# Where two pieces of work stand at the entry of a halved FFN: values of two covered tiles, and ScalarE's copy of a bank

## The chip, the cores and the metric

The kernel runs on one core of one Trainium2 chip. The metric is the time of one execution on the device in microseconds (us), as the median of several executions; lower is better. Engines are called TensorE (PE in the profile: matmuls, PEld its weight loads), VectorE (DVE), ScalarE (ACT), GpSimd (POOL) and SyncE (SP, which issues most DMAs).

## The reference, cut to what matters

The reference is a two-layer decoder trunk on one sequence of 512 tokens with 1024 features, in float32. Each layer has two SwiGLU FFNs, one on each side of a block of three token mixers, so an execution runs four FFNs.

```python
D_MODEL = 1024
SEQ = 512
DEPTH = 2
D_FF = 2816

def rms_norm(x, gain):
    xf = x.astype(jnp.float32)
    inv = lax.rsqrt(jnp.mean(xf * xf, axis=-1, keepdims=True) + EPS)
    return (xf * inv).astype(x.dtype) * gain

def swiglu(h, w_in, w_out):
    gate, up = jnp.split(h @ w_in, 2, axis=-1)
    return (jax.nn.silu(gate) * up) @ w_out

    for l in range(DEPTH):
        x = x + 0.5 * swiglu(rms_norm(x, ffn1_norm[l]), ffn1_w_in[l], ffn1_w_out[l])
        ...
        x = x + y @ w_mix_out[l]
        x = x + 0.5 * swiglu(rms_norm(x, ffn2_norm[l]), ffn2_w_in[l], ffn2_w_out[l])
```

## The kernel before, in words

Every float32 product is made of three matmuls on rounded operands: an operand is split into a high part (rounded by ScalarE) and a low part, the remainder (a subtraction by VectorE), and `mm3` (L304) issues high times high, high times low of the moving side, low of the weights times high (L308, L314, L315).

An FFN has 22 tiles of 128 hidden features, taken in pairs, in three chunks of 8, 8 and 6 tiles (`CHUNKS`). The first `covered` tiles (6 in the first FFN, 4 in the others) are computed plainly, on x times the gain, while the norm is still being computed: `enter` (L541) does it for the last three FFNs, `cover` (L474) for the first. Their banks are taken out by `clear` (gate and up times the norm's factor `inv` on VectorE, then Silu on ScalarE) and `values` (two VectorE instructions per tile, L669 and L666, that multiply gate and up into the hidden tile `hq`).

All other tiles are computed by `halved` (L722) in a scheme with seven products, named P1 to P7, in place of eight (Strassen and Winograd's). A unit is one pair of tiles (kind "I", the input projection) or one half of the output projection of one of the first two chunks (kind "O"; the last chunk is projected plainly); there are 35 units of kind I in an execution. A product is 24 matmuls into one of three banks of its unit. In a unit of kind I the order is P1, P2, P6, P5, P7, P3, P4: P1, P6, P7 and P4 accumulate one after the other in bank a, P2 fills bank c, P5 and P3 accumulate in bank b. Between two products of a bank it has to be read:

- P1: ScalarE copies bank a, negated, to g1 (L865); P2: VectorE subtracts bank c from g1 (L868), ScalarE takes Silu;
- P6: ScalarE copies bank a, negated, to g2 (L872); P5: ScalarE copies bank b, negated, to u2 (L875);
- P7: VectorE adds bank a to u2 (L878); P3: VectorE adds bank b to g2 (L881), ScalarE takes Silu;
- P4: VectorE multiplies up the two hidden tiles out of g2, u2 and g1, bank a (L669, L666; L895, L896 in the last chunk).

So P6's copy must end before P7 can start, with P5 between; P5's copy before P3, with P7 between; and L878 before P4, with P3 between.

`plan` (L60) writes down one sequence of products per FFN: the first units of kind I alone, then I mixed with O. `LEAD` is 3: when product n has been issued, `prepare` rounds the weights (one granule of 128 x 1024, tile `hl`, three buffers) for product n+3 on ScalarE (L766), and hands back a function, `rest`, that has VectorE form the remainder (L768). This rounding writes the buffer that product n has just read. The body of the loop (L839 to L910) issues for each n: the product, the rounding of n+3, the reading of n's bank, `rest`, the list of sums and loads that the plan puts at n (`run(n)`; sums on VectorE L754, L780), and, in the first products of an FFN, one entry of `self.entry`, with which `enter` spreads its remaining work.

The order on each engine is the order in which these lines are issued: `follow` (L268) ties each of these instructions to the one before it on the same engine (`A` for ScalarE, `V` for VectorE). What `enter` does before the first halved product ends with the sum of the inputs of P7 (`add((0, 1), (1, 1))`), and `next(then)`, which lets `halved` go to its first products. The inputs of the products are formed by `high` (ScalarE, L589) and `low` (VectorE, L592 or L594) of tiles `xn`, into `xc`.

Of the kernel before, what the change touches and what calls it, by code (L numbers as in the profile page):

```python
# [13 lines left out]
AF = mybir.ActivationFunctionType  # L14
# [142 lines left out]
class Trunk:  # L157
# [377 lines left out]
    def values(self, fp, f, i, gi, ui, keep):  # L535
        V = (lambda i: self.follow("v", i)) if keep else (lambda i: i)
        a, k = divmod(f + i, 4)
        for b in range(2):
            V(self.hidden(self.quarter(fp, 0, a, b)[:, k, :], *(t[:, 256 * b : 256 * b + 256] for t in (gi, ui)), a != b))

    def enter(self, fp, w_in, then):  # L541
        nc = self.nc
        H = T // 2
        A, V = (lambda i, e=e: self.follow(e, i) for e in "av")

        def stream(f, banks, given):
            def parts(k, kk):
                r = slice(k * P, (k + kk) * P)
                return [w_in[r, f * P : (f + 2) * P], w_in[r, FF + f * P : FF + (f + 2) * P]]

            return self.stream_steps(
                [(bk, slice(c, c + P), None) for bk, c in zip(banks, (0, 256, 128, 384))],
                parts, self.xact, KD, given=given,
            )

        ba = self.next4()
        first = stream(0, ba, lambda k: k == KD - 2)
        for _ in range(4):
            next(first)
        nb = self.bank("pt" if self.ntog % 2 == 0 else "po")  # L560
        bb = self.next4()
        second = stream(2, bb, lambda k: True)
        self.ngain = self.const.tile([P, KD], F32, tag="ngain", name=self.n("ngain"))
        A(nc.scalar.activation(self.ngain, self.gain, AF.Copy, scale=-1.0))
        next(second)
        self.end_norm(nb, fp, True)
        self.table(SILU)
        next(first, None)
        next(then)
        X, self.xc, lows = {}, {}, {}  # L570

        def quarter(a, b):
            X[a, b] = t = fp.tile([P, 4, H], F32, tag=f"r{2 + 2 * a + b}", name=self.n("xn"))
            for k in range(4):
                i = 4 * a + k
                V(nc.vector.scalar_tensor_tensor(
                    out=t[:, k, :], in0=self.xT[:, i, b * H : (b + 1) * H],
                    scalar=(self.gain if a == b else self.ngain)[:, i : i + 1],
                    in1=self.inv[:, b * H : (b + 1) * H], op0=ALU.mult, op1=ALU.mult,
                ))  # L580

        def high(name):
            c = ORDER_IN.index(name)
            src, other = X[SUM[name]], name in NEGATIVE
            hi, lo = (
                fp.tile([P, 4, H], F32R, tag=f"x{w}{c}", name=self.n("xc")) for w in "hl"
            )
            self.xc[name] = hi, lo
            A(nc.scalar.activation(hi, src, AF.Copy, scale=-1.0) if other else nc.scalar.copy(hi, src))  # L589

            def low():
                V(nc.vector.scalar_tensor_tensor(  # L592
                    out=lo, in0=src, scalar=-1.0, in1=hi, op0=ALU.mult, op1=ALU.subtract
                ) if other else nc.vector.tensor_sub(lo, src, hi))  # L594

            lows[name] = low

        def add(x, y):
            V(nc.vector.tensor_add(X[x], X[x], X[y]))

        def both(name):
            high(name)
            lows[name]()

        def row():
            next(second)
            next(second, None)

        cleared = {}

        def clear(f, i):
            banks = bb if f else ba
            cleared[f, i] = self.clear(fp, banks[2 * i], banks[2 * i + 1], True)

        def values(f, i):
            self.values(fp, f, i, *cleared.pop((f, i)), True)

        quarter(0, 0)
        high("P1")
        quarter(1, 0)  # L620
        lows["P1"]()
        next(second)
        next(second)
        high("P2")
        quarter(0, 1)
        lows["P2"]()
        quarter(1, 1)
        next(second)
        next(second)
        add((0, 0), (0, 1))  # L630
        high("P5")
        clear(0, 0)
        lows["P5"]()
        next(second)
        next(second)
        next(second, None)
        add((0, 0), (1, 1))
        high("P6")
        self.given["total"]()
        lows["P6"]()  # L640
        self.given["prepare"](0)
        self.given["prepare"](1)
        clear(0, 1)
        add((0, 1), (1, 1))
        next(then)
        self.entry = {
            0: lambda: (high("P7"), values(0, 0), lows["P7"]()),
            1: lambda: (values(0, 1), high("P3")),
            2: lambda: (lows["P3"](), add((0, 0), (1, 0))),
            3: lambda: both("P4"),  # L650
            9: lambda: clear(2, 0),
            10: lambda: values(2, 0),
            12: lambda: clear(2, 1),
            13: lambda: values(2, 1),
        }
# [66 lines left out]
    def halved(self, fp, w_in, w_out, covered):  # L722
        nc = self.nc
# [3 lines left out]
        A, V, G, S = (lambda i, e=e: self.follow(e, i) for e in "avgs")  # L727
# [13 lines left out]
        def add(u, q, q2):  # L741
            G(nc.gpsimd.dma_start(raw[u, q], src(u, q2), accum_op=ALU.add))
# [70 lines left out]
        u = seq[0][:2]  # L813
# [25 lines left out]
        for n, (kind, w, p) in enumerate(seq):  # L839
# [3 lines left out]
            if p in new:  # L843
# [3 lines left out]
                u, p, acc, p in new, p in ("P2", "P3", "P4"),  # L847
                kind == "I" and p == "P1" and w in (covered, *(f0 for f0, _ in CHUNKS)),
            )
            rest = prepare(*seq[n + LEAD]) if n + LEAD < len(seq) else None  # L850
            if kind == "O":
                c, g = w

                for r, b, f in {
                    "P2": ((0, 0, -0.5),), "P1": ((0, 0, -0.5),), "P5": ((1, 1, -0.5),),
                    "P6": ((0, 1, -0.5),), "P7": ((1, 1, 0.5),), "P3": ((0, 1, 0.5),),
                    "P4": ((1, 0, 0.5),),
                }[p]:
                    xs = self.xT[:, 4 * r + 2 * g : 4 * r + 2 * g + 2, b * H : (b + 1) * H]
                    V(nc.vector.scalar_tensor_tensor(  # L860
                        out=xs, in0=pair(acc), scalar=f, in1=xs, op0=ALU.mult, op1=ALU.add
                    ))
            elif p == "P1":
                work[u, "g1"] = g1 = tmp("g1")
                A(nc.scalar.activation(g1, acc, AF.Copy, scale=-1.0))  # L865
            elif p == "P2":
                g1 = work[u, "g1"]
                V(nc.vector.tensor_sub(g1, g1, acc))  # L868
                A(self.act(g1, g1, AF.Silu))
            elif p == "P6":  # L870
                work[u, "g2"] = g2 = tmp("g2")
                A(nc.scalar.activation(g2, acc, AF.Copy, scale=-1.0))  # L872
            elif p == "P5":
                work[u, "u2"] = u2 = tmp("u2")
                A(nc.scalar.activation(u2, acc, AF.Copy, scale=-1.0))  # L875
            elif p == "P7":
                u2 = work[u, "u2"]
                V(nc.vector.tensor_add(u2, u2, acc))  # L878
            elif p == "P3":
                g2 = work[u, "g2"]  # L880
                V(nc.vector.tensor_add(g2, g2, acc))  # L881
                A(self.act(g2, g2, AF.Silu))
            else:
                g1, g2, u2 = (work[u, x] for x in ("g1", "g2", "u2"))
                c = next(i for i, (f0, nf) in enumerate(CHUNKS) if f0 <= w < f0 + nf)
                if c < 2:
                    a, k = divmod(w - CHUNKS[c][0], 4)
                    for b, g, v in ((1, g2, u2), (0, g1, acc)):
                        V(self.hidden(
                            self.quarter(fp, c, a, b)[:, k : k + 2, :], pair(g), pair(v), a != b  # L890
                        ))
                else:
                    q = (w - CHUNKS[c][0]) // 2
                    y = fp.tile([P, 2, T], F32, tag="S", name=self.n("y"), bufs=2)
                    V(nc.vector.tensor_mul(y[:, :, H:], pair(g2), pair(u2)))  # L895
                    V(nc.vector.tensor_mul(y[:, :, :H], pair(g1), pair(acc)))  # L896
                    hh, hl = (
                        fp.tile([P, 2, T], F32R, tag=f"r{t}", name=self.n("hh")) for t in tags[q]
                    )
                    self.hh.append(hh)  # L900
                    self.hl.append(hl)
# [718 lines left out]
```

## Time and profile before

| | |
|---|---|
| median of 3 runs | 1860.53 us (1856.95 to 1863.77) |
| profiled execution, its own time | 1854.12 us |
| its span, first to last instruction | 1852.3 us |
| TensorE clock granted | 1.00 |
| instructions | 33371 |

How to read the rows that follow. A row of the timeline has the start in us from the span's beginning, the duration, engine, line of the kernel, operation, output and input tiles (buffer numbers left out), shape, count, and in brackets how long the engine was idle before and what ended it. A row of the waits has who waited, for whom, us in total, how many times, and the longest. Rows of one engine overlap a little: an instruction starts before the last one has drained.

### The profile page before, as it was taken

To read this page: it belongs to the slowest core of one execution; us is meant where nothing else is said; L and a number is where in the kernel's file an instruction comes from. 1 tells how busy PE (TensorE), PEld (TensorE's weight loads), DVE (VectorE), ACT (ScalarE), POOL (GpSimd) and SP (SyncE) were. 2 spreads that over 40 slices of the span, in tenths; PEclk is the share of its full clock that TensorE was granted. 3 is DMA by queue.
4 is the path that set the end of the run, shared out by engine and by line. 5 is a ranking of instruction groups with operands and counts; after the bars stand their busy time and mean duration, and the time that the engine had idled before them with its cause. 6 is when DMAs were issued, how large, how long until landed. Compare 5 with 4: busy or idle time off the path is not lost.

```text
span 1852.3 us, 33371 instructions
## 1 busy us (share of the span) xinstructions
PE 1829.1 (99%) x13536; PEld 1700.0 (92%) x13536; DVE 1480.2 (80%) x2101; ACT 1007.3 (54%) x1467; POOL 177.3 (10%) x182
## 2 busy tenths in 40 slices
PE   8999999999999999999999999999999999999999
PEld 6899999899877899999889999998998788999997
DVE  7889787678787888878678887966868878888883
ACT  5455555564665555555445555545546664555552
POOL 0011120100000001112001111201000000020210
PEclk9999999999999999999999999999999999999999
DMA  7658783232223767868265787813323228577762
GB/s 205 171 121 190 182 176 96 69 95 73 75 75 97 209 131 170 186 170 171 81 200 127 163 192 185 171 59 90 81 64 87 80 91 228 148 160 194 150 136 91
DMA packets 245417, 251.90 MB, mean 136 GB/s; under 512 B 19568, under 2 KB 230000, under 8 KB 245264
## 3 DMA queue, kind: packets, MB, share of 16 engines
q1 hardware_dynamic: 191664, 183.69, 32.5%
q0 software_dynamic: 53600, 66.09, 22.3%
q8 instruction: 106, 1.74, 0.4%
q14 instruction: 47, 0.39, 0.1%
HBM read 223.98 MB, written 2.10 MB: 122 GB/s over the span
## 4 chain that ended last, share of the span: by engine, by line
PE 88%; DVE 6%; ACT 3%; issue 2%; DMA 1%; SPq 0%; ACTq 0%; DVEq 0%
PE mm L308 13%; PE mm L315 13%; PE mm L314 13%; PE sc L308 6%; PE sc L315 6%; PE sc L314 6%; PE pt L308 6%; PE pt L314 6%; PE pt L315 6%; PE po L308 3%; PE po L314 3%; PE po L315 3%; PE po L1472 1%; DVE hl L298 1%; PE pt L1513 1%
## 5 line engine op out<-in xcount | busy, mean ns | idle before, releaser
L766 ACT CAST hl<-w 128x1024 fp32r<-128x1024 f32 x322 | 337.2, 1049 | 317.2 <-PE mm L315 76.5
L768 DVE TENSOR_TENSOR hl<-w,hl 128x1024 fp32r<-128x1024 f32 x322 | 392.8, 1222 | 90.8 <-ACT hl L766 90.7
L298 DVE TENSOR_TENSOR hl<-st,hl 128x512 fp32r<-128x512 f32 (+2 forms) x196 | 166.5, 852 | 114.7 <-ACT hl L297 113.6
L297 ACT CAST hl<-st 128x512 fp32r<-128x512 f32 (+2 forms) x196 | 146.6, 750 | 184.8 <-PE mm L315 66.7
L308 PE MATMUL mm<-xc,hl 128*128 128x256 f32 (+1 forms) x732 | 201.7, 276 | 1.7 <-ACT g L872 1.4
L315 PE MATMUL mm<-xc,hl 128*128 128x256 f32 x728 | 201.4, 277 | 0.0
L314 PE MATMUL mm<-xc,hl 128*128 128x256 f32 x728 | 201.4, 277 | 0.0
L308 PE MATMUL sc<-xc,hl 128*128 128x256 f32 (+1 forms) x530 | 146.6, 277 | 2.4 <-ACT g L872 1.7
L315 PE MATMUL sc<-xc,hl 128*128 128x256 f32 x528 | 146.3, 277 | 0.0
L314 PE MATMUL sc<-xc,hl 128*128 128x256 f32 x528 | 146.2, 277 | 0.0
L308 PEld LDWEIGHTS mm<-xc,hl 128*128 128x128 f32 x732 | 137.4, 188 | 2.5 <-ACT g L872 1.8
L315 PEld LDWEIGHTS mm<-xc,hl 128*128 128x128 f32 x728 | 136.7, 188 | 0.1
L314 PEld LDWEIGHTS mm<-xc,hl 128*128 128x128 f32 x728 | 136.7, 188 | 0.0
L308 PE MATMUL pt<-xc,hl 128*128 128x256 f32 (+1 forms) x484 | 133.0, 276 | 0.0
L314 PE MATMUL pt<-xc,hl 128*128 128x256 f32 x480 | 133.0, 277 | 0.0
L315 PE MATMUL pt<-xc,hl 128*128 128x256 f32 x480 | 132.8, 277 | 0.0
L308 PE MATMUL mm<-hl,x 128*128 128x256 f32 (+1 forms) x384 | 112.3, 292 | 0.7 <-DVE qk L1403 0.3
L308 PE MATMUL mm<-x,hl 128*128 128x512 f32 x272 | 109.7, 403 | 0.0
L315 PE MATMUL mm<-hl,x 128*128 128x256 f32 (+1 forms) x384 | 107.4, 280 | 0.0
L314 PE MATMUL mm<-hl,x 128*128 128x256 f32 (+1 forms) x384 | 107.1, 279 | 0.0
L315 PE MATMUL mm<-x,hl 128*128 128x512 f32 x272 | 106.5, 392 | 0.0
L314 PE MATMUL mm<-x,hl 128*128 128x512 f32 x272 | 106.0, 390 | 0.0
(478 smaller groups left out, 5678.2 us busy)
## 6 DMA issues: line engine op xcount, KB each, us to landing
w<-in_ffn_w_in_dram SPq DMA_DIRECT2D x140, 512.0 KB, 5.5
w<-in_ffn_w_out_dram SPq DMA_DIRECT2D x64, 512.0 KB, 4.2
w<-in_ffn_w_out_dram POOLq DMA_DIRECT2D x56, 512.0 KB, 8.6
st<-in_w_mix_in_dram SPq DMA_DIRECT2D x88, 256.0 KB, 2.7
st<-in_ffn_w_in_dram SPq DMA_DIRECT2D x72, 256.0 KB, 3.1
w<-in_ffn_w_in_dram POOLq DMA_DIRECT2D x35, 512.0 KB, 8.5
w<-S POOLq DMA_DIRECT2D x35, 512.0 KB, 4.7
st<-in_ffn_w_out_dram SPq DMA_DIRECT2D x24, 512.0 KB, 3.6
```

The lines of the kernel that those rows point to most:

```text
L297: a = nc.scalar.copy(hi, src[:, c : c + w])
L298: b = nc.vector.tensor_sub(lo, src[:, c : c + w], hi)
L308: i = nc.tensor.matmul(acc[:, c], ah, bh[:, c], start=first and c.start == 0, stop=False, skip_group_check=True,)
L314: nc.tensor.matmul(acc, ah, bl, start=False, stop=False, skip_group_check=True)
L315: i = nc.tensor.matmul(acc, al, bh, start=False, stop=last, skip_group_check=True)
L766: A(nc.scalar.copy(hi, src))
L768: return lambda: V(nc.vector.tensor_sub(lo, src, hi))
L1472: nc.tensor.matmul(self.ob[:, t0 + u * P : t0 + 2 * P], V[:, j, h % 4].rearrange("p a d -> p (a d)"), part[:, j, u:, :].rearrange("p i t - ...
L1513: nc.tensor.transpose(tb[:, j * P : (j + 1) * P], p[:, j * P : (j + 1) * P], self.ident)
```

## The change

In `enter`, `values` of the second pair of covered tiles' first two tiles, (0, 0) and (0, 1), is issued before `next(then)`; before, it was part of the entries of products 0 and 1. With that, the input of P7 is formed in one piece after product 0, and the input of P3 in one piece after product 2, where its high part was issued after product 1.

In `halved`, the three copies of a bank by ScalarE (P1 to g1, P6 to g2, P5 to u2) are issued before `prepare` of product n+3, where they stood behind it. This holds for every unit of kind I, in all four FFNs.

```diff
@@ enter
         clear(0, 1)
         add((0, 1), (1, 1))
+        values(0, 0)
+        values(0, 1)
         next(then)
         self.entry = {
-            0: lambda: (high("P7"), values(0, 0), lows["P7"]()),
-            1: lambda: (values(0, 1), high("P3")),
-            2: lambda: (lows["P3"](), add((0, 0), (1, 0))),
+            0: lambda: both("P7"),
+            2: lambda: (both("P3"), add((0, 0), (1, 0))),
             3: lambda: both("P4"),
             9: lambda: clear(2, 0),
             10: lambda: values(2, 0),
@@ halved
+            out = {"P1": "g1", "P6": "g2", "P5": "u2"}.get(p) if kind == "I" else None
+            if out is not None:
+                work[u, out] = t = tmp(out)
+                A(nc.scalar.activation(t, acc, AF.Copy, scale=-1.0))
             rest = prepare(*seq[n + LEAD]) if n + LEAD < len(seq) else None
             if kind == "O":
                 c, g = w
@@
-            elif p == "P1":
-                work[u, "g1"] = g1 = tmp("g1")
-                A(nc.scalar.activation(g1, acc, AF.Copy, scale=-1.0))
+            elif out is not None:
+                pass
             elif p == "P2":
                 g1 = work[u, "g1"]
                 V(nc.vector.tensor_sub(g1, g1, acc))
                 A(self.act(g1, g1, AF.Silu))
-            elif p == "P6":
-                work[u, "g2"] = g2 = tmp("g2")
-                A(nc.scalar.activation(g2, acc, AF.Copy, scale=-1.0))
-            elif p == "P5":
-                work[u, "u2"] = u2 = tmp("u2")
-                A(nc.scalar.activation(u2, acc, AF.Copy, scale=-1.0))
             elif p == "P7":
                 u2 = work[u, "u2"]
                 V(nc.vector.tensor_add(u2, u2, acc))
```

## The prediction

> **What bounds the kernel now.** First the busy times of the page, then the list of what TensorE waited for.
>
> ```profile
> PE 1829.1 (99%) x13536; PEld 1700.0 (92%) x13536; DVE 1480.2 (80%) x2101; ACT 1007.3 (54%) x1467; POOL 177.3 (10%) x182
> ...
> PE sc L308 <- ACT g L872: 1.7, 2, 0.9
> PE mm L308 <- ACT g L872: 1.4, 2, 0.9
> PE sc L308 <- DVE u L878: 0.7, 2, 0.4
> PE mm L308 <- DVE u L878: 0.3, 1, 0.3
> ```
>
> TensorE is busy 99% of 1852.3 us; a change that removes no matmul can only close its gaps. The last four rows are all the waits that the halved products have for ScalarE's bank copies (L872, four times) and for VectorE's evacuation L878 (three times): once per FFN at its entry, for L878 in the last three FFNs only. They add up to 4.1 us of idle time, 0.2% of the span. So the upside is small from the start, and the question is what the new order makes late elsewhere.
>
> Second, the timeline of one entry (second FFN; the third and fourth repeat it), ScalarE, VectorE and TensorE in order of time.
>
> ```profile
> 650.70 0.59 ACT L865 ACTIVATE g<-sc 128x512 f32<-128x512 f32 x1
> 650.83 1.23 DVE L768 TENSOR_TENSOR hl<-w,hl 128x1024 fp32r<-128x1024 f32 x1 [1.62 <-ACT hl L766]
> 653.11 0.42 DVE L669 TENSOR_TENSOR hq<-gi,ui 128x256 f32<-128x256 f32 x1
> 653.78 1.22 DVE L592 SCALAR_TENSOR_TENSOR xc<-xn,xc 128x1024 fp32r<-128x1024 f32 x1
> 654.91 0.68 DVE L868 TENSOR_TENSOR g<-g,sc 128x512 f32<-128x512 f32 x1
> 655.63 0.64 ACT L262 ACTIVATE g<-g 128x512 f32<-128x512 f32 x1 [1.27 <-DVE g L868]
> 656.17 1.04 ACT L589 CAST xc<-xn 128x1024 fp32r<-128x1024 f32 x1
> 657.11 1.04 ACT L766 CAST hl<-w 128x1024 fp32r<-128x1024 f32 x1
> 657.55 0.28 PE L315 MATMUL pt<-xc,hl 128*128 128x256 f32 x1
> 658.05 0.59 ACT L872 ACTIVATE g<-sc 128x512 f32<-128x512 f32 x1
> 658.18 1.23 DVE L768 TENSOR_TENSOR hl<-w,hl 128x1024 fp32r<-128x1024 f32 x1 [0.78 <-ACT hl L766]
> 658.69 0.39 PE L308 MATMUL sc<-xc,hl 128*128 128x256 f32 x1 [0.87 <-ACT g L872]
> 663.95 0.68 DVE L878 TENSOR_TENSOR u<-u,sc 128x512 f32<-128x512 f32 x1
> 664.78 0.36 PE L308 MATMUL sc<-xc,hl 128*128 128x256 f32 x1 [0.35 <-DVE u L878]
> ```
>
> Starts give the steps, since an engine's rows overlap by some 0.1: 0.54 us for the Silu (655.63 to 656.17, its row is 0.64 long), 0.94 for a rounding (656.17 to 657.11), so 0.49 for a bank copy (0.59 less 0.10), and 0.67 for one call of values, two instructions (653.11 to 653.78). P7 accumulates into the bank that P6's copy reads. The last matmul before it starts at 657.55 and the rows around it are 0.11 apart, so P7 was wanted at 657.66 and came at 658.69: 1.03 lost, because the copy stood behind two roundings. P4 then waits for L878, which ends at 664.63; it starts 0.15 later.
>
> **The change, part by part.** No instruction is added or removed; TensorE, GpSimd and SyncE keep their order, and no DMA is moved. Two things move: in 35 units the three copies (P1, P6, P5) each go past one rounding on ScalarE, so a copy comes up to 0.94 sooner and that rounding up to 0.49 later; and in three entries 4 VectorE instructions of values (1.34 us) go ahead of the remainder of P6's granule, and the rounding of P3's input (656.17) goes behind two more ScalarE instructions. A copy put in front adds no wait on ScalarE: it waits for the end of its product, and the rounding behind it fills the buffer which that same product read. What stands behind the rounding is VectorE's remainder of it, and behind that the rest of VectorE's list; that is where the 0.49 can hurt. P3's input, 1.3 us later, is covered: its remainder came after VectorE's row of 658.18 in any case, and P3 follows P7 by a product.
>
> Entry of FFNs 2 to 4, the 1.03 at P7. VectorE idled 1.62 before its row at 650.83, waiting for the rounding that P1's copy now precedes: +0.49. One call of values no longer stands in front of L868: -0.67. L868 starts at 654.73, the Silu at 655.45, P6's copy right behind it at 655.99, done by 656.58, before 657.66. The wait is gone. The 1.34 us of values in front of P6's remainder fit into the 1.62 of idle time; without that they would cost P6 directly.
>
> The same entry, P4. P3's weights are now rounded at 656.48 instead of 657.11, so VectorE's row of 658.18 (it idled 0.78 there) moves to 657.55. From there to L878 VectorE runs without a pause, so L878 also moves by 0.63 and P4 starts at 664.15 instead of 664.78. Of the 1.03 only 0.63 are left; P4 waits 0.5 longer than it did.
>
> The next unit and a half. Here these rows decide.
>
> ```profile
> 679.34 0.63 ACT L262 ACTIVATE gi<-gi 128x512 f32<-128x512 f32 x1 [1.40 <-DVE gi L530]
> 679.88 1.03 ACT L766 CAST hl<-w 128x1024 fp32r<-128x1024 f32 x1
> 680.94 1.22 DVE L768 TENSOR_TENSOR hl<-w,hl 128x1024 fp32r<-128x1024 f32 x1 [1.04 <-ACT hl L766]
> 689.16 0.68 DVE L666 SCALAR_TENSOR_TENSOR hq<-g,pt 128x512 f32<-128x512 f32 x1
> 690.30 0.28 PE L308 MATMUL pt<-xc,hl 128*128 128x256 f32 x1
> ```
>
> The Silu at 679.34 hangs on VectorE, which by then runs only about 0.16 earlier (each copy-first slot eats 0.49 of the 0.63). Behind it P5's copy now comes before the rounding: 679.88 - 0.16 + 0.49 = 680.21. VectorE, idle there for 1.04, starts its row at 681.27 instead of 680.94 and runs without a pause to L666, which ends at 690.17 instead of 689.84. L666 empties the bank that P2 of the third unit takes. That P2 stood at 690.30, would be wanted at 689.67, and gets its bank at 690.17 + 0.15 = 690.32. The remaining gain is used up: +0.02 per entry, together **+0.1**. Bounds: if the 0.33 doesn't appear, -0.63 each; if the copies of that unit add a whole 0.49, +0.2.
>
> Entry of the first FFN, where values doesn't move.
>
> ```profile
> 86.13 1.23 DVE L768 TENSOR_TENSOR hl<-w,hl 128x1024 fp32r<-128x1024 f32 x1 [1.62 <-ACT hl L766]
> 91.55 0.63 ACT L262 ACTIVATE gi<-gi 128x512 f32<-128x512 f32 x1 [1.36 <-DVE gi L530]
> 92.08 1.03 ACT L766 CAST hl<-w 128x1024 fp32r<-128x1024 f32 x1
> 93.02 0.58 ACT L872 ACTIVATE g<-mm 128x512 f32<-128x512 f32 x1
> 93.66 0.39 PE L308 MATMUL mm<-xc,hl 128*128 128x256 f32 x1 [0.53 <-ACT g L872]
> 94.58 1.23 DVE L768 TENSOR_TENSOR hl<-w,hl 128x1024 fp32r<-128x1024 f32 x1 [0.20 <-ACT hl L766]
> 98.16 0.68 DVE L878 TENSOR_TENSOR u<-u,mm 128x512 f32<-128x512 f32 x1
> 99.22 0.28 PE L308 MATMUL mm<-xc,hl 128*128 128x256 f32 x1
> ```
>
> P1's copy ahead of a rounding moves VectorE's row of 86.13, and all that hangs on it up to the Silu of 91.55, by 0.49. P6's copy follows it at 92.57 instead of 93.02, so P7 starts 0.45 sooner, at 93.21. The rounding behind that copy moves from 92.08 to 93.06, and the next one, behind P5's copy, by as much: VectorE's row of 94.58 (idle before it, so ScalarE sets it) moves to 95.56, L878 ends at 99.82 instead of 98.84, and P4 starts at 99.97 instead of 99.22: **+0.75**. Bounds: -0.45 if VectorE catches up, +0.98 if the slack of 0.23 isn't there.
>
> The end of every FFN. A third place has no wait in the list, but no slack either.
>
> ```profile
> 247.58 1.05 ACT L766 CAST hl<-S 128x1024 fp32r<-128x1024 f32 x1 [2.65 <-DVE S L754]
> 254.53 0.63 ACT L262 ACTIVATE g<-g 128x512 f32<-128x512 f32 x1 [1.44 <-DVE g L868]
> 255.06 1.03 ACT L766 CAST hl<-w 128x1024 fp32r<-128x1024 f32 x1
> 256.13 1.23 DVE L768 TENSOR_TENSOR hl<-w,hl 128x1024 fp32r<-128x1024 f32 x1 [0.50 <-ACT hl L766]
> 261.28 1.23 DVE L768 TENSOR_TENSOR hl<-w,hl 128x1024 fp32r<-128x1024 f32 x1 [0.36 <-ACT hl L766]
> 282.30 1.05 ACT L766 CAST hl<-S 128x1024 fp32r<-128x1024 f32 x1 [3.29 <-DVE S L754]
> 283.38 1.23 DVE L768 TENSOR_TENSOR hl<-S,hl 128x1024 fp32r<-128x1024 f32 x1 [1.19 <-ACT hl L766]
> 284.67 0.38 PE L315 MATMUL mm<-xc,hl 128*128 128x256 f32 x1
> ```
>
> This is the last unit but one and the last unit (first FFN; the other three have the same pattern). The third matmul of P6 in the last unit, at 284.67, reads the remainder that VectorE ends at 283.38 + 1.23 = 284.61: slack 0.06. That remainder hangs on ScalarE's rounding at 282.30, which hangs on a VectorE sum, which ends a stretch that VectorE works from 261.28 with no pause that isn't its own doing. P1's copy in either unit costs nothing: it falls into ScalarE's idle 2.65 and 3.29. P6's copy does not: it comes between the Silu at 254.53 and the rounding at 255.06, for which VectorE waits (0.50). Row 256.13 moves by 0.49; row 261.28 moves by 0.49 too, once only, since P5's copy, in front of its rounding, does the same in parallel. The 0.49 go through to 284.67. Four FFNs: **+2.0**. Bounds: 0 if a pause that I take for a dependence is slack; 0.98 each, 3.9, if P6's and P5's copies add.
>
> Everywhere else a rounding works two products ahead, and the 0.49 is covered by those two products, 5.56 us (93.66 to 99.22). Sum: 0.1 + 0.75 + 2.0 = **+2.8**. The profiled execution took 1854.12 us (span 1852.3 and 1.8 around it), so it would take 1856.9. It lies 6.4 below the median 1860.53 of the runs; the change is put on the median: **1863.3**.
>
> P6's bank, filled a product before 657.66, waited until 658.05 to be read. The Trainium skill, page "PSUM — Partial Sum Buffer", section "Summary: rules for kernel authors", says to evacuate promptly; by that rule the copy belongs in front, and the sum would be the waits of the first list given back. The trace agrees that the copy was late; that the time stays won is what it doesn't show, and this is the first rival.
>
> **The rivals.** *Prompt copies keep their gain.* For it: all four waits on L872 go away or shrink. Then each of three entries gives back 1.03 at P7 and 0.5 at P4, and the first one the 0.53 of its row: -5.1, 1855.4. Against it: VectorE, at 80% of the span, runs from 658.18 to 663.95 without a pause. Chance 0.12.
>
> *Slower: VectorE's backlog at the end of the FFN adds up.* If the idle 0.50 and 0.36 before 256.13 and 261.28 are used up by work that slides in, the copies of both last units (P6, P5, P6) delay the same chain one after another, 3 x 0.49 = 1.5 in each FFN, 5.9, with the entries' 0.85 +6.7: 1867.2. It decides as soon as VectorE reaches 261.28 with no idle time left. For it: the slack of 0.06. Against it: the copies of P6 and P5 fall on different pauses. Chance 0.20.
>
> *The change does nothing that reaches TensorE's end*: the tail absorbs its 0.49 and the entries cancel, 1860.5. For it: TensorE shows no wait of the tail's kind in the list. Chance 0.18.
>
> **How the numbers follow.** Forecast 0.50, rivals 0.12, 0.20, 0.18. The bounds of the forecast's own terms add up to -2.3 and +5.1, 1858.2 to 1865.6. The runs of before spread over 6.8 us, so a median moves by some 3 either way; with the cases' 1855 to 1867 the range is 1856 to 1868. What can be told from no change is 0.3%, 5.6 us. Faster by more: a third of the first rival and a little scatter, 0.05. Slower by more: two thirds of the second rival and a tenth of the forecast, 0.19. Within: 0.76.
>
> **What would show it.** In the trace of after, the waits on the P6 copy should be gone in FFNs 2 to 4 and about 0.25 long in the first; the wait for u (P7's evacuation) should appear in all four FFNs, about 1 us from start to start in FFNs 2 to 4. P2 of the third unit should start within 0.1 us of where it did, counted from P1 of the first. The third matmul of P6 in each last unit should be about 0.5 late. Wrong: an entry that is shorter by over 0.6, a tail without the 0.5, or a new wait on a moving tile or a DMA.

## The result, and the profile after

| | before | after |
|---|---|---|
| median of 22 runs each, us | 1861.4 | 1866.9 |
| lowest to highest, us | 1854.1 to 1866.1 | 1857.0 to 1872.9 |
| profiled execution: span (its own time), us | 1852.3 (1854.1) | 1857.0 (1858.8) |

The ratio after to before is 1.0026, with a 95% interval of 1.0015 to 1.0038: some 5 us slower (the medians differ by 5.5). That lies just inside the 0.3% that the prediction counted as no change, though the interval reaches beyond it. Forecast were 1863.3 and +2.8.

First, the busy times and the list of TensorE's waits in the profile after (us in total, times, longest).

```profile
PE 1832.4 (99%) x13536; PEld 1702.4 (92%) x13536; DVE 1476.6 (80%) x2101; ACT 1007.0 (54%) x1467; POOL 177.3 (10%) x182
...
PE sc L308 <- DVE u L876: 1.6, 2, 0.8
...
PE mm L308 <- DVE u L876: 1.5, 2, 0.8
...
PE mm L315 <- DVE hl L769: 0.5, 2, 0.3
PE sc L315 <- DVE hl L769: 0.5, 2, 0.3
...
PE pt L308 <- ACT hl L767: 0.4, 1, 0.4
PE po L308 <- DVE hq L667: 0.4, 1, 0.4
PE pt L308 <- DVE hq L667: 0.4, 1, 0.4
```

The waits for ScalarE's bank copies are gone from the list. In their place stand four waits for u (VectorE's evacuation of P7, now L876), four new ones at the third matmul of a product (L315, at the ends of the FFNs), and three at P2 of the third unit in FFNs 2 to 4 (the last three rows, into pt or po). The copies are now L854, the roundings L767, their remainders L769; the second of the two instructions that empty a unit's bank a is L667 (L666 before).

Second, the entry of FFN 2, in order of time.

```profile
658.53 0.58 ACT L854 ACTIVATE g<-sc 128x512 f32<-128x512 f32 x1
660.25 0.28 PE L308 MATMUL sc<-xc,hl 128*128 128x256 f32 x1
665.85 0.68 DVE L876 TENSOR_TENSOR u<-u,sc 128x512 f32<-128x512 f32 x1
666.67 0.36 PE L308 MATMUL sc<-xc,hl 128*128 128x256 f32 x1 [0.81 <-DVE u L876]
682.22 0.58 ACT L854 ACTIVATE u<-sc 128x512 f32<-128x512 f32 x1
682.70 1.04 ACT L767 CAST hl<-w 128x1024 fp32r<-128x1024 f32 x1
683.77 1.23 DVE L769 TENSOR_TENSOR hl<-w,hl 128x1024 fp32r<-128x1024 f32 x1 [1.52 <-ACT hl L767]
691.98 0.68 DVE L667 SCALAR_TENSOR_TENSOR hq<-g,pt 128x512 f32<-128x512 f32 x1
692.80 0.36 PE L308 MATMUL pt<-xc,hl 128*128 128x256 f32 x1 [0.42 <-ACT hl L767]
```

P6's copy ends at 659.11, before P7 starts at 660.25 without a wait. P4 waits at 666.67 for L876, which ended 0.14 earlier. P5's copy of the second unit (682.22) stands ahead of the rounding at 682.70, VectorE's idle time before the remainder has grown from 1.04 to 1.52, and P2 of the third unit starts at 692.80, 0.14 after L667 has emptied its bank. (The list puts this one wait down to ScalarE's rounding, and the same wait in FFNs 3 and 4 to L667. P2 starts equally close behind the end of L667 in all three, so it is L667 that it waits for.)

Third, the last unit of FFN 1: the first three matmuls of P6, before,

```profile
284.43 0.28 PE L308 MATMUL mm<-xc,hl 128*128 128x256 f32 x1
284.54 0.28 PE L314 MATMUL mm<-xc,hl 128*128 128x256 f32 x1
284.67 0.38 PE L315 MATMUL mm<-xc,hl 128*128 128x256 f32 x1
```

and after, with the remainder that the third one reads.

```profile
285.80 1.22 DVE L769 TENSOR_TENSOR hl<-S,hl 128x1024 fp32r<-128x1024 f32 x1 [1.17 <-ACT hl L767]
...
286.43 0.28 PE L308 MATMUL mm<-xc,hl 128*128 128x256 f32 x1
286.54 0.28 PE L314 MATMUL mm<-xc,hl 128*128 128x256 f32 x1
287.08 0.39 PE L315 MATMUL mm<-xc,hl 128*128 128x256 f32 x1 [0.26 <-DVE hl L769]
```

The third matmul starts 0.65 after the first; before it was 0.24. So the end of this FFN is 0.41 longer.

Counted from the first product of each FFN, starts of products in the two traces differ as follows (a plus is later in after):

| start of | FFN 1 | FFN 2 | FFN 3 | FFN 4 |
|---|---|---|---|---|
| P7 of the first unit | -0.50 | -1.03 | -1.04 | -1.04 |
| P4 of the first unit | +0.38 | -0.70 | -0.69 | -0.71 |
| FFN 1: P1 of the second unit; FFNs 2 to 4: P2 of the third | +0.47 | -0.09 | -0.11 | -0.08 |
| third matmul of P6 in the last unit, counted from its first | +0.42 | +0.39 | +0.41 | +0.36 |

The product behind that P2 gives the 0.09 back, so the entries of FFNs 2 to 4 come out at nothing. Both executions have the same stretch of slower matmuls (told of below) between P4 and the third unit in these three FFNs, so it cancels here. The sum is 0.47 + 0.0 + 1.6 = 2.1 us. The spans differ by 4.7. Of the rest 1.5 lie in the opening, ahead of the first FFN, which the change doesn't touch: the first product of FFN 1 starts at 81.95 in this one profile of before, and at 83.36 in the profile of before with a few matmuls split (below), at 83.47 in after. Another 0.9 is a stretch at the end of FFN 3 whose matmuls follow each other 118 ns apart instead of 113; 0.2 lie between the FFNs. Such stretches turned out to be what spreads the runs.

### The profile page after: what moved, and what is told of

The parts are those of the page before. It is cut to its first block, busy times and chain, and to the rows that moved or that the text cites. A ratio compares the mean times of both kernels' runs of the same rounds, so it can differ in the third digit from the quotient of the medians.

```text
span 1857.0 us, 33366 instructions
## 1 busy us (share of the span) xinstructions
PE 1832.4 (99%) x13536; PEld 1702.4 (92%) x13536; DVE 1476.6 (80%) x2101; ACT 1007.0 (54%) x1467; POOL 177.3 (10%) x182
## 4 chain that ended last, share of the span: by engine, by line
PE 82%; DVE 10%; ACT 4%; issue 3%; DMA 1%; SPq 0%; ACTq 0%; DVEq 0%
PE mm L308 12%; PE mm L315 12%; PE mm L314 12%; PE sc L315 5%; PE sc L308 5%; PE sc L314 5%; PE pt L308 5%; PE pt L314 5%; PE pt L315 5%; PE po L308 3%; PE po L314 3%; PE po L315 3%; DVE hl L769 2%; ACT hl L767 1%; PE po L1470 1%
## 5 line engine op out<-in xcount | busy, mean ns | idle before, releaser
L767 ACT CAST hl<-w 128x1024 fp32r<-128x1024 f32 x322 | 336.9, 1047 | 260.7 <-PE mm L315 64.7
L769 DVE TENSOR_TENSOR hl<-w,hl 128x1024 fp32r<-128x1024 f32 x322 | 393.0, 1221 | 105.1 <-ACT hl L767 104.5
L315 PE MATMUL mm<-xc,hl 128*128 128x256 f32 x728 | 201.5, 277 | 0.5 <-DVE hl L769 0.5
L315 PE MATMUL sc<-xc,hl 128*128 128x256 f32 x528 | 146.3, 277 | 0.5 <-DVE hl L769 0.5
L315 PEld LDWEIGHTS mm<-xc,hl 128*128 128x128 f32 x728 | 136.7, 188 | 0.9 <-DVE hl L769 0.9
L315 PE MATMUL pt<-xc,hl 128*128 128x256 f32 x480 | 132.8, 277 | 0.0
L315 PE MATMUL mm<-hl,x 128*128 128x256 f32 (+1 forms) x384 | 107.4, 280 | 0.0
L315 PE MATMUL mm<-x,hl 128*128 128x512 f32 x272 | 106.6, 392 | 0.0
```

Of the source, the lines that this page charges most:

```text
L315: i = nc.tensor.matmul(acc, al, bh, start=False, stop=last, skip_group_check=True)
L767: A(nc.scalar.copy(hi, src))
L769: return lambda: V(nc.vector.tensor_sub(lo, src, hi))
```

## The experiments

**Each part alone, the tail undone, and the change again.** `values` alone, that is the first part of the change (the two tiles moved are those of the first covered pair):

```diff
+        values(0, 0)
+        values(0, 1)
...
-            0: lambda: (high("P7"), values(0, 0), lows["P7"]()),
-            1: lambda: (values(0, 1), high("P3")),
-            2: lambda: (lows["P3"](), add((0, 0), (1, 0))),
+            0: lambda: both("P7"),
+            2: lambda: (both("P3"), add((0, 0), (1, 0))),
```

> The four VectorE instructions of values stand ahead of the first halved product, ScalarE's copies stay behind the rounding. Theory (the copies cost, values help): in FFNs 2 to 4 the subtraction of P2's bank comes 0.67 us sooner, so P7 starts without a wait and P4 about 1.3 us sooner than before; nothing moves at the first FFN's entry or at the ends of the FFNs. Together -3.9 us, ratio to before 0.998. Rival (values in front of the remainder of P6's granule is what costs): P6 or P5 starts late by up to 1.3 us in three FFNs, up to +4 us, ratio 1.002.

Measured: ratio 0.9975 (0.9964 to 0.9985), median 1851.05 against 1855.28.

```profile
659.30 0.28 PE L308 MATMUL sc<-xc,hl 128*128 128x256 f32 x1
664.27 0.68 DVE L879 TENSOR_TENSOR u<-u,sc 128x512 f32<-128x512 f32 x1
665.10 0.36 PE L308 MATMUL sc<-xc,hl 128*128 128x256 f32 x1 [0.19 <-DVE u L879]
```

In this timeline of FFN 2 P7 (659.30) starts without a wait although P6's copy stands behind its rounding as before; counted from P1 it is 1.03 earlier, and P4 1.32 earlier (18.13 to 16.81). So the gain at P7 needs only values; moving the copies wasn't needed for it.

The copies alone, and the whole change with the copies of the last two units left behind the rounding:

```diff
...
-            rest = prepare(*seq[n + LEAD]) if n + LEAD < len(seq) else None
+            rest = None
+            for what in ("copy", "round") if kind == "O" or w < 18 else ("round", "copy"):
+                if what == "copy" and out is not None:
+                    work[u, out] = t = tmp(out)
+                    A(nc.scalar.activation(t, acc, AF.Copy, scale=-1.0))
+                if what == "round" and n + LEAD < len(seq):
+                    rest = prepare(*seq[n + LEAD])
```

> The copies of P1, P6 and P5 stand ahead of the rounding in every unit, values stay where they were before. Theory: +0.5 us at the first FFN's entry, +0.45 at the end of each FFN, and in FFNs 2 to 4 the entry loses about 0.9 us each, since the subtraction of P2's bank then comes 0.5 later and nothing makes up for it: together +4 to +5.5 us, ratio 1.002 to 1.003, slower than the whole change in the trace of its entries. Rival (values cost): faster than the whole change, within 1 us of before.

> The whole change, but in the last two units of each FFN (tiles 18 to 21) the copies stay behind the rounding. Theory: the 0.45 us at the end of each FFN is gone (-1.8 us against the whole change), the entries are those of the whole change: +0.5 us against before, ratio 1.000. Rival (the end of the FFN is late for another reason, such as a DMA): the end still loses 0.4 us or more in each FFN.

> The whole change once more. Theory: the same steps between marks as in its first trace (first FFN's entry +0.47 us, entries of FFNs 2 to 4 zero in sum, ends of the FFNs +0.41 to +0.48 each, 2.2 us in all), within 0.05 us; what differs from trace to trace is the opening before 60 us and stretches in which matmuls follow each other 118 ns apart in place of 113. Rival (the 4.7 us between the first two traces are all of the change): the opening and the fourth product from the end of the third FFN are late again by 1.5 and 0.75 us.

Measured: the copies alone 1.0086 (1.0071 to 1.0101), 1871.2 us, far above what was expected; without the tail 1.0036 (1.0024 to 1.0048), where 1.000 was expected; the change again 1.0053 (1.0031 to 1.0075), 1859.9 to 1873.6. The repeat's trace has the steps of the first at the entry of FFN 1 (+0.46) and at the ends (+0.36 to +0.42); its entries of FFNs 2 to 4 come out otherwise, as told under the prediction. Its opening is late again (84.30; the other traces of this document lie between 81.95 and 83.70, with either order of the copies), and it has a stretch of nine products at the end of each FFN. Without the tail the third matmul of P6 stands 0.24 after the first again in all four FFNs, so that step is undone as expected. But in its trace, from P2 of the third unit of FFN 4 on, 41 products had their matmuls 118 ns apart, 2.83 us a product instead of 2.72, 4.4 us in all. With the copies alone this happened in FFNs 2, 3 and 4. Here is the same stretch of FFN 4 in the windows of the copies alone and of the next experiment (length; busy us and instructions of each engine; granted clock; DMA).

```profile
core 0: us, PE busy (x) PEld busy (x) DVE busy (x) ACT busy (x) POOL busy (x), PEclk, DMA share, GB/s
...
1640.00:1745.00 105.00, 105.00 (x896) 105.00 (x896) 84.75 (x88) 52.28 (x60) 16.55 (x14) 1.00 0.73 163
```

```profile
1640.00:1745.00 105.00, 105.00 (x929) 105.00 (x928) 87.05 (x90) 56.05 (x64) 14.49 (x13) 1.00 0.83 191
```

896 matmuls against 929 in the same 105 us, with TensorE 100% busy and the granted clock at 1.00 both times: no list of waits and no clock row shows it, only the count.

**What ends such a stretch.** In every trace so far the stretches that outlast one product went on to a product whose first matmul is made in two halves (P1 of the first unit of a chunk), or to the last halved product of the FFN. So one more product is split in this way, P6 of the unit that begins with tile 8 (w = 8 in the code, the third unit of FFNs 2 to 4), right behind the late P2; the copies alone otherwise.

```diff
-                kind == "I" and p == "P1" and w in (covered, *(f0 for f0, _ in CHUNKS)),
+                kind == "I" and (p == "P1" and w in (covered, *(f0 for f0, _ in CHUNKS)) or (w, p) == (8, "P6")),
```

> The three copies ahead of the rounding and nothing else of the change, as in the run of that alone (1.0086), and in addition the first matmul of P6 of the unit w = 8 (the product right behind the late P2) made in two halves, as P1 of some units already is. That run showed, from the late P2 of the third unit on, 41 products of FFNs 2, 3 and 4 with their matmuls 118 ns apart instead of 113: 2.827 us instead of 2.72 each, 4.4 us per FFN. Theory (a split matmul ends such a stretch): the stretches end with the product that is split, 12.9 us of some 15 go, ratio 1.002 to 1.003. Rival (the spacing is set by time, heat or clock, and the split P1s only stand where it ends by itself): the stretches stay, ratio 1.008 to 1.009. A third: the split itself costs more than some 0.05 us a time, then the products behind it show it.

Measured: 1.0024 (1.0012 to 1.0037), 1862.0 to 1864.5 us, where the copies alone had 1868.1 to 1877.3; the span went from 1875.6 to 1860.2, as the theory had it. The timeline of TensorE in FFN 4 shows the end of a stretch.

```profile
1611.19 0.28 PE L314 MATMUL pt<-xc,hl 128*128 128x256 f32 x1
...
1613.78 0.28 PE L315 MATMUL pt<-xc,hl 128*128 128x256 f32 x1
1613.90 0.33 PE L308 MATMUL pt<-xc,hl 128*128 128x128 f32 x2
1614.07 0.33 PE L314 MATMUL pt<-xc,hl 128*128 128x256 f32 x1
1614.24 0.28 PE L315 MATMUL pt<-xc,hl 128*128 128x256 f32 x1
...
1616.62 0.28 PE L315 MATMUL pt<-xc,hl 128*128 128x256 f32 x1
```

From 1611.19 to 1613.78 there are 22 steps of 118 ns. Then comes the split matmul (x2), and from 1614.24 to 1616.62 there are 21 steps of 113 ns. With the copies alone the stretch that began at this P2 went on past P6, for 41 products in all, in each of FFNs 2 to 4; here it ends with the split, at a granted clock of 1.00 on both sides. This trace has only one stretch at P2; the three profiles with three splits (below) have eleven more products behind a wait at 118 ns, and the split product behind each of them is back at 113.

The same with values alone, with P1 of the second unit of FFNs 2 to 4 split:

> values moved, the copies as before (the run of that alone gave 0.9975), and in addition the first matmul of P1 of the second unit of FFNs 2 to 4 in two halves; in FFN 1 nothing changes. In the trace of values alone the second to the seventh product after P4's wait had their matmuls 118 ns apart in FFNs 2 and 3, until the split P1 of the unit w = 8. Theory (a split matmul ends the stretch): P1 of the second unit is back at 113, 7 products gain 0.107 each, 0.75 per FFN where it occurs, ratio 0.996 to 0.997. Rival (the stretch ends by itself after some 20 us or at a chunk's start): 0.9975 as without the split, and the 118 ns go on to the same place.

Measured: in the trace the stretch that starts at P4 is down from eight products to P4 alone (FFNs 2 and 4), as expected, but the run times spread from 1851.6 to 1864.8 and the ratio is 0.9992 (0.9974 to 1.0011), where 0.996 to 0.997 was expected: inconclusive for the median. Other stretches were left; the profiled execution had one at the end of FFN 1.

**Which copy makes P2 of the third unit late.** The whole change, with P5's copy of the second unit behind the rounding in FFNs 2 to 4:

```diff
+            late = p == "P5" and w == covered + 2 and covered != FIRST
...
+            for what in ("round", "copy") if late else ("copy", "round"):
...
```

> The whole change, but in FFNs 2 to 4 P5's copy of the second unit stays behind the rounding. Theory of the prediction (that copy takes back the 0.33 that P4 left over): VectorE's row behind that rounding comes 0.33 to 0.49 sooner, L667 ends by as much sooner, and P2 of the third unit waits 0.2 at most instead of 0.6: each entry 0.4 to 0.6 shorter than in the changed kernel, 1.2 to 1.8 us in all, and no stretch of 118 ns behind P2, since the wait that starts it is gone or short. Rival (P2 waits because of P1's and P6's copies of the two units, P5's adds nothing): P2 waits 0.6 as before, ratio as in the changed kernel, 1.003 to 1.005.

```profile
683.50 1.23 DVE L769 TENSOR_TENSOR hl<-w,hl 128x1024 fp32r<-128x1024 f32 x1 [1.04 <-ACT hl L767]
...
691.72 0.68 DVE L667 SCALAR_TENSOR_TENSOR hq<-g,pt 128x512 f32<-128x512 f32 x1
...
692.54 0.36 PE L308 MATMUL pt<-xc,hl 128*128 128x256 f32 x1
```

Measured: VectorE's idle time is back at 1.04. Counted from P1 of the first unit, P2 starts at 42.74 in FFN 2. After has 43.56 there, but with the products behind P4 at 118 ns, which this execution hasn't; the repeat of the change, without that stretch too, has 43.22. So P5's copy costs P2 0.48, inside the 0.4 to 0.6 expected. P2 stands 0.14 behind the end of L667 (691.72 + 0.68) and 0.23 behind the matmul before it, so the wait is down to 0.12 (in the kernel before it is 0.11, in executions without the stretch behind P4). No long stretch started at P2. The ratio, 1.0002 (0.9983 to 1.0021), fits both a gain and none.

**Which copy makes the end of the FFN late.** One copy of the last unit but one (w = 18) at a time, in the kernel before: P6's, then P5's.

```diff
...
+            for what in ("copy", "round") if kind == "I" and w == 18 and p == "P6" else ("round", "copy"):
...
```

> The kernel before, but in the last unit but one (w = 18) of each FFN P6's copy goes ahead of the rounding; no other copy and no values is moved. Theory (the prediction's step for the end of the FFN): the third matmul of P6 in the last unit starts 0.41 to 0.49 later in each of the four FFNs, 1.6 to 2.0 us in the span, as in the changed kernel. Rival (it needs P5's or P1's copy as well, or a copy of the last unit): below 0.1 each.

> The kernel before, but in the last unit but one (w = 18) of each FFN P5's copy goes ahead of the rounding; no other copy and no values is moved. With P6's copy alone in front, the third matmul of P6 in the last unit came only 0.01, 0.03, 0.26 and 0.19 us later in the four FFNs; the 0.49 in front of the first VectorE row was taken up by the idle time of 0.36 ahead of the next one. Theory now (it is P5's copy that delays that chain): 0.40 to 0.49 at each end, as in the changed kernel. Rival (only the copies of P6 and P5 together use the idle time up): below 0.15 each. The spacing of 118 ns may come and go behind it by 0.75 or 4.4 a time, and isn't counted.

FFN 1 with P6's copy in front:

```profile
257.98 1.23 DVE L768 TENSOR_TENSOR hl<-w,hl 128x1024 fp32r<-128x1024 f32 x1 [0.99 <-ACT hl L766]
...
261.54 2.36 DVE L768 TENSOR_TENSOR hl<-w,hl 128x1024 fp32r<-128x1024 f32 x2 [0.59 <-ACT hl L766]
...
285.80 0.28 PE L308 MATMUL mm<-xc,hl 128*128 128x256 f32 x1
...
286.05 0.39 PE L315 MATMUL mm<-xc,hl 128*128 128x256 f32 x1
```

and with P5's copy in front:

```profile
256.69 1.23 DVE L768 TENSOR_TENSOR hl<-w,hl 128x1024 fp32r<-128x1024 f32 x1 [0.50 <-ACT hl L766]
...
262.27 1.23 DVE L768 TENSOR_TENSOR hl<-w,hl 128x1024 fp32r<-128x1024 f32 x1 [0.80 <-ACT hl L766]
...
284.99 0.29 PE L308 MATMUL mm<-xc,hl 128*128 128x256 f32 x1
...
285.66 0.38 PE L315 MATMUL mm<-xc,hl 128*128 128x256 f32 x1 [0.26 <-DVE hl L768]
```

P6's copy moves the first remainder by 0.49 (idle 0.99 instead of 0.50), but the idle 0.36 ahead of a later one vanishes (two remainders follow each other, x2), and the third matmul stands 0.25 behind the first, as before. In FFNs 3 and 4 it stands 0.5 behind; why these differ is open. (Each of the two was run once, so only its trace is used, not its time.) P5's copy raises the later idle time from 0.36 to 0.80, and the third matmul stands 0.67 or 0.68 behind the first in all four FFNs. P5's copy alone costs what the whole change costs there.

**The change without the stretches.** In the kernel before, in after and in values alone three products per FFN are split (two in FFN 1), one behind each place where a product waits:

```diff
-                kind == "I" and p == "P1" and w in (covered, *(f0 for f0, _ in CHUNKS)),
+                kind == "I" and (
+                    p == "P1" and w in (covered, *(f0 for f0, _ in CHUNKS))
+                    or (w, p) in ((8, "P6"), (20, "P5")) or p == "P1" and (covered, w) == (4, 6)
+                ),
```

> The kernel before, with three more first matmuls made in two halves: P1 of the second unit in FFNs 2 to 4, P6 of the unit w = 8, and P5 of the last unit. Each lies right behind a place where a product waits. Theory (the spread of the runs of before, 1854 to 1869, is stretches of 118 ns that start at such a wait in some executions and not in others, 4.4 or 0.75 us each): stretches end within two products, the runs lie within 3 us of each other, median 1852 to 1854.5, ratio 0.995 to 0.998. Rival (the spread has another origin): spread as before.

> The changed kernel with the same three splits. Theory (the change itself costs what its waits add up to, 0.47 at the first entry, nothing at the others, 0.4 at each end, 2.2 us; the rest of the measured difference is 118 ns stretches that its new wait at P2 of the third unit starts): 1.5 to 3 us slower than before with the same splits, 1854 to 1857, spread under 3 us. Rival (the rest comes from elsewhere): 4 to 7 us slower than before with the same splits.

> values moved, the copies as before, with the same three splits. Theory: 3.5 to 4 us faster than before with the same splits (1.03 at P7 and 0.2 to 0.3 at P4 in each of three entries), 1848 to 1851, ratio to the kernel before 0.994 to 0.997, spread under 3 us: the fastest of all. Rival: as values alone, 0.9975 or above.

| with three splits | median, us | lowest to highest | ratio to before without them (95% interval) |
|---|---|---|---|
| before | 1855.54 | 1854.8 to 1856.3 | 0.9991 (0.9982 to 1.0000) |
| after | 1858.93 | 1857.9 to 1859.9 | 1.0011 (1.0001 to 1.0020) |
| values alone | 1851.77 | 1850.9 to 1852.1 | 0.9969 (0.9957 to 0.9981) |

The 24 runs of before without splits, on the same chip in the same session, went from 1853.4 to 1863.5. The spread of 10 us becomes 1.5, and in the three profiles no stretch outlasts one product: the spread was that of the stretches, in before too. The medians lie 0.8 to 1.9 us above what was expected of them; a split costs some 0.13 us itself (a product of 2.85 us instead of 2.72), so the median of before gains only 0.9. Free of the stretches the change costs 1858.93 - 1855.54 = 3.4 us, a little over the 1.5 to 3 expected. In the profiles of the two the four FFNs of after, from the first halved product to the last, are 0.86, 0.69, 0.83 and 0.73 us longer, 3.1 together. values alone gains 1855.54 - 1851.77 = 3.8. It beats both kernels with the splits (0.9969) as without them (0.9975); the intervals of the two overlap, and the splits mainly make its runs agree.

## Why the prediction was right, and where it was not

*The wait at P7 goes away: right.* -1.03 in FFNs 2 to 4, as counted. In FFN 1 -0.50 against -0.45; of the wait there 0.19 are left from start to start, too short for the list, where about 0.25 was forecast.

*P4 gives part of it back: right.* 0.70 earlier than before, counted from P1, against 0.63. It waits for u in all four FFNs; in FFN 2 it starts 1.09 behind the matmul before it, 0.98 more than the usual step. Before that was 0.51 more, so it waits 0.47 longer; the prediction wrote 0.5, though its own 1.03 and 0.63 leave 0.40.

*P5's copy uses up the rest by P2 of the third unit: right, and shown.* P2 was to stand within 0.1 of where it stood; it stands 0.08 to 0.11 earlier. Without P5's copy in front it comes 0.48 earlier, the 0.49 that the step put on that copy. But the +0.02 holds only for executions like the two profiled ones, whose products between P4 and the third unit ran at 118 ns; that both were of this kind is luck. In executions without that stretch P2 starts 42.93 behind P1 in the kernel before (the runs with one copy of the tail moved, where the entry is untouched) and 43.22 in the repeat of the change: +0.3 per entry. The upper bound of this step was also added up too low: 0.18 an entry (0.49 - 0.33 + 0.02) make 0.5 in three, not 0.2.

*Entry of FFN 1, +0.75: the right mechanism, too large.* P4 starts 0.38 later, the product behind it 0.47. The step that failed is that all of the 0.98 would pass from VectorE's remainder at 94.58 to L878. A pause between them, not shown in the prediction, took up 0.32. In before, and then in after:

```profile
97.49 0.42 DVE L666 SCALAR_TENSOR_TENSOR hq<-gi,ui 128x256 f32<-128x256 f32 x1 [0.48 <-ACT gi L262]
```

```profile
97.03 1.23 DVE L769 TENSOR_TENSOR hl<-w,hl 128x1024 fp32r<-128x1024 f32 x1 [0.21 <-ACT hl L767]
...
99.62 0.42 DVE L667 SCALAR_TENSOR_TENSOR hq<-gi,ui 128x256 f32<-128x256 f32 x1 [0.16 <-ACT gi L262]
...
101.12 0.36 PE L308 MATMUL mm<-xc,hl 128*128 128x256 f32 x1 [0.73 <-DVE u L876]
```

With the opening's 1.52 taken off, the remainder moved by 0.93 and L666 by 0.61; its idle time shrank from 0.48 to 0.16. 0.75 - 0.32 is 0.43, between the 0.38 and the 0.47 measured.

*The end of each FFN, +0.49: the right size, from the wrong copy.* Measured 0.36 to 0.42. The prediction had P6's copy do it and P5's "in parallel"; alone, P6's does nothing in FFNs 1 and 2 and about half in FFNs 3 and 4, and P5's does all of it. That the size came out all the same is in part luck. The two don't add, as the prediction had it against its second rival: together they cost no more than P5's alone. The prediction also let the whole 0.49 through although it read a slack of 0.06 there; 0.43 is nearer to what was measured.

*The sum, +2.8.* By the steps of the two profiled executions it is 2.1; with the stretches cut off in both kernels the medians differ by 3.4 (0.47 + 3 x 0.3 + 1.6 = 3.0 of it are the steps named here); and the medians of the first comparison differ by 5.5. The median of 1866.9 lies near the upper end of the range of 1856 to 1868, and some 2 of the 5.5 us are of a kind that no term of the sum held; that the range took them in is the scatter it allowed for, not its mechanism. What the prediction lacked is a term for the time between two matmuls. It took a wait's price to be its length. P2's new wait stands right behind the split P1 that used to end the stretch begun at P4; where a stretch starts there, it runs on for 41 products, 4.4 us. The runs of after spread from 1857.0 to 1872.9, with the three splits (in another session) from 1857.9 to 1859.9. What decides in which execution a stretch starts is open: the length of the wait doesn't, since P2 came 0.70 behind the matmul before it in the profile of after, and 0.85 in the repeat, without a stretch, while with one copy of the tail moved in before it came 0.22 behind, as it does in before, and a stretch of 41 products started there in one FFN of each run.

*The rivals.* "Prompt copies keep their gain" fell: with the copies alone and one split the runs were 0.24% slower than a before that still had its stretches, and in the profiles without long stretches (this one, and before with three splits) the four FFNs are some 6.6 us longer together. The Trainium skill, page "PSUM — Partial Sum Buffer", section "Summary: rules for kernel authors", says to evacuate promptly. By the copies alone P7 did start 0.5 us sooner, but P4 started 0.92 later in FFNs 2 to 4 (19.05 behind P1 instead of 18.13). The entry of FFN 2 in that run, where u is evacuated by L875:

```profile
662.00 1.23 DVE L768 TENSOR_TENSOR hl<-w,hl 128x1024 fp32r<-128x1024 f32 x1 [1.26 <-ACT hl L766]
667.77 0.68 DVE L875 TENSOR_TENSOR u<-u,sc 128x512 f32<-128x512 f32 x1
668.60 0.36 PE L308 MATMUL sc<-xc,hl 128*128 128x256 f32 x1 [1.30 <-ACT hl L766]
```

The row of P4 names the rounding. But P4 starts 0.15 behind the end of L875 in FFNs 2 to 4 alike, as it starts 0.15 behind u's evacuation wherever it waits in before and in after; and the weights that P4 reads were rounded three products earlier. So it waits for u. The rounding that the copy delays acts through VectorE: VectorE waits 1.26 for it before its remainder (0.78 before the change), and from there to L875 it runs without a pause.

"The backlog adds up at the end" and "nothing reaches TensorE's end" fell too, by the 0.4 in each FFN. The 1867.2 of the backlog rival is close to the measured median, but its mechanism is not what happened.

## What to carry to other kernels

ScalarE here serves two readers with one queue, in the order in which the kernel issues: before an evacuation is moved ahead of a cast, look for who reads the cast, and for the idle time ahead of that reader which says that it is already waiting. The wait that named the copy was cured by taking 1.34 us of other work out of VectorE's way, with the copy where it was. A wait that the list puts down to one engine is best held against the rows: here P2 and P4 started 0.15 behind the end of a VectorE row while the list named ScalarE. And where runs of a kernel spread by more than its waits explain, count the matmuls in equal windows of two runs before explaining the difference by the change.

## What the runs showed of the hardware that was not expected

TensorE's back-to-back matmuls of 128x128 by 128x256 go at 113 ns from start to start, and in some stretches at 118 (929 against 896 in 105 us) at a granted clock of 1.00. A stretch starts behind a wait in some executions and not in others. Those that outlast one product lasted until a matmul was made in two halves (128 and 128 columns) or until the last halved product of the FFN, up to 41 products of 24 matmuls. Splitting three first matmuls per FFN (two in FFN 1) took the spread of the runs from 10 us to 1.5.
